# Attention's group ends spread over three steps, output products between its last transposes, and a reordered start of the gate products

## The chip, the cores and the metric

The kernel runs on one core of a Trainium2 chip. A core has five engines with an instruction queue each: TensorE (matrix products and transposes; the profile calls it PE, and its weight loads PEld), VectorE (DVE), ScalarE (ACT), GpSimd (POOL) and SyncE (SP, which here issues DMAs). Each engine works through its queue in order, and waits where an operand or a buffer is not ready. The metric is the device time of one execution in microseconds (us); the median of several runs is compared.

## The reference

The program computes one layer of a hybrid encoder block in float32, on 1024 tokens of width 1024:

```python
h = rms_norm(x, norm1_g)
a, gate, q, k, v = split(h @ w_in)                  # 512 columns each
conv_out = silu(layer_norm(depthwise_conv31(a * sigmoid(gate)) + dw_bias))
q, k = rms_norm per head (8 heads of 64) of q, k
attn_out = neighbourhood_attention(q, k, v, rpb)    # 16 x 64 token grid, window 8 rows x 16 columns
x = x + concat([conv_out, attn_out]) @ w_out
h = rms_norm(x, norm2_g)
out = x + (silu(h @ w_gate) * (h @ w_up)) @ w_down  # hidden width 2816
```

## The kernel before

Every large product is made from two rounded parts of each operand. `split(hi, lo, src, sub)` lets ScalarE write the rounded copy `hi`, and then the engines in `sub` write the remainder `lo = src - hi`, each an equal share of the columns; GpSimd is the default. `mac` (lines 110 to 114) then runs three matrix products on TensorE: hi with hi, hi with lo, lo with hi. The order of the work is written out by hand: each function issues instructions, and each engine takes its own in that order. A list `woven` holds functions that are called one by one between the products of a running accumulation (`weave`).

**Attention** works in 32 steps, one pair of heads of one query block each; four steps make a group (`order`), a group has one half of the rows (`rh`) and one block of 16 columns (`cb`). The loop (from line 775) is a software pipeline. Step i makes the scores of pair i (`score_mm`, TensorE; `score_exp`, VectorE and ScalarE), scales the exponentials of pair i - 1 (`score_norm`: reciprocal on VectorE, scaling on GpSimd), transposes those of pair i - 2 (`flip`, into the one buffer `cv` of PSUM, emptied by `flip_out`: one half by ScalarE, then the other by VectorE), and multiplies the transposed ones of pair i - 3 with the values (`weigh`, into `os_`, one bank for a group, two such banks). When the fourth pair of a group has been weighed (step 6, 10, 14, ...), `evac` splits the group's output into `at`, ScalarE first and then VectorE. Columns of the groups are 24 wide at first (288 scores a row) and 32 wide from step 16 (384 scores).

Beside this, `take_parts` cuts the split of a piece of output weights `wo` into four quarters, `jobs`, one called at the end of every second step: ScalarE's rounded copy and GpSimd's remainder. `take` does a whole piece at once. After the fourth quarter the next piece is loaded (SyncE's queue).

At step 32, `attn_half(0)` runs the four attention blocks (k = 4 to 7) of the output product of token block 0, 12 matrix products in a row, ahead of the last two transposes. After the loop follow the convolution's transposes `conv_T` (the first into `cv`), the rest of the output products, and `conv_stats`, which takes means and variances on VectorE, in part with operations on 128x1 numbers (lines 739 and 747).

**From the output product to the gate.** The second half of the output product runs over eight token blocks t (from line 984): products, `resid(t, 1)` (VectorE adds the residual), `norm2(t)` (a DMA of the sum, ScalarE's square and root). Woven into the next block's products are `norm2_out(t - 1)` (VectorE scales to `xn`), the transposes `t2_one` with their splits into `h2`, and `s_sum`.

The gate and up products are made by a Strassen scheme: seven products m1 to m7 of half-sized blocks for each of 22 blocks i (`FB`), instead of eight. `s_sum(t, ns, eng)` makes the sums S1, S2 (`sn`) and, in place, S3 and S4 (in `xn`) of the tokens; `t_sums` those of the weights on VectorE; `s_T` transposes and splits a sum of the tokens into four blocks. `prep` takes the next (i, p) of `tasks`, makes the weight's sum where needed, splits it (remainder on GpSimd) and issues loads of later weights. `product(i, p)` runs 12 matrix products; `evac(i, p, acc)` empties or combines the result. Three products share bank A or B or D: m2 of a block goes into the bank that its m1 used, so it waits for the copy of m1 into `g` (line 1020, ScalarE). The first two blocks are interleaved: m1 of block 0, m1 of block 1, m2 of block 0, m2 of block 1, then m6, m5, m7, m4, m3 in the same way. After the eighth token block and ahead of the first product stand `norm2_out(7)`, an activation that makes ScalarE load the table for Silu (line 995), `s_sum(3, (1, 2), dve)` and one `prep`.

Of the kernel before, what the change touches and what calls it, by code (L numbers as in the profile page):

```python
# [6 lines left out]
F32 = mybir.dt.float32  # L7
# [60 lines left out]
def build(ctx, tc, a):  # L68
# [25 lines left out]
    def mm(name):  # L94
        return ps.tile([P, 512], F32, tag="mm", bufs=4, name=name)
# [7 lines left out]
    def split(hi, lo, src, sub=(pool,)):  # L103
        act.copy(hi, src)  # L104
        n = src.shape[-1] // len(sub)
        for i, eng in enumerate(sub):
            sl = slice(i * n, (i + 1) * n)
            eng.tensor_tensor(*[w[..., sl] for w in (lo, src, hi.bitcast(F32))], OP.subtract)  # L108
# [8 lines left out]
    woven = []  # L117
# [71 lines left out]
    def wo_dst(d, k0):  # L189
        def dst():  # L190
            if (d, k0 // 4) not in woq:
                woq[d, k0 // 4] = H(f"wo{d}{k0}", F32R)
            q = woq[d, k0 // 4]
            o = k0 % 4 * 1024
            hl = (q[:, o:o + 1024], q[:, o + 1024:o + 2048])
            for j in range(2):
                wo[d, k0 + j] = [w[:, j * 512:(j + 1) * 512] for w in hl]
            return hl
        return dst

    for d in range(2):
        for k0 in (4, 6, 0, 2):
            want(a["wo"][k0 * P:(k0 + 2) * P, d * 512:(d + 1) * 512].rearrange("(k p) m -> p k m", p=P),
                 f"wo{d}{k0}", wo_dst(d, k0))


    hT = [[H(f"hT{h}{w}", F32R).rearrange("p (k s) -> p k s", s=512) for w in range(2)] for h in range(2)]
# [442 lines left out]
    def weigh(i):  # L650
        s_, hp = divmod(i, 4)
        rh, cb = order[s_]
        if hp == 0:
            os_[s_] = tp(f"o{s_}").rearrange("p (c q) -> p c q", c=4)
        for g in range(3):
            for hh in range(2):
                c = (2 * hp + hh) * HD
                pe.matmul(os_[s_][hh * HD:(hh + 1) * HD, hp], vw[cb, rh + g][:, c:c + HD], pTs[i][:, g, hh],  # L658
                          start=g == 0, stop=g == 2)

    def evac(s_):
        rh, cb = order[s_]
        o = os_.pop(s_)
        if rh == 0:
            at[cb] = [G(f"at{cb}{w}", F32R).rearrange("p (c t q) -> p c t q", c=4, t=2) for w in range(2)]
        split(*[w[:, :, rh] for w in at[cb]], o, (dve,))

    def value(t):
        z = nat(2, t)
# [42 lines left out]
    def proj(t, d, acc, ks):  # L712
        for k in ks:
            mac(acc, lhs(k, t), wo[d, k], k == 4, k == 3)
            weave()

    def conv_T(t):
        y = cv(f"y{t}")[:, :512] if t in (0, 3) else tp(f"y{t}")
        for c in range(4):
            pe.transpose(y[:, c * P:(c + 1) * P], u[c][0][:, t * P:(t + 1) * P], ident)  # L720
        return y
# [3 lines left out]
    def conv_stats(t, y):  # L725
        st6, mv, sd = SM(f"bs{t}", 6), SM(f"bm{t}", 2), SM(f"bd{t}", 1)
        dve.bn_stats(st6, y)
        dve.bn_aggr(mv, st6)
        act.activation(sd, mv[:, 1:2], AF.Sqrt, bias=eps)
        cs[t] = y, mv, sd  # L730
        if 1 <= t <= 4:
            conv_scale(t - 1)
        if t >= 4:
            conv_scale(t)
# [36 lines left out]
    def attn_half(t):  # L771
        acc0.append(mm(f"pj{t}"))
        proj(t, 0, acc0[t], range(4, 8))

    for i in range(2, 32 + 2):
        if i == 5:
            tab[0, 1] = tab[0, 2] = table(0, 1)
        if i == 9:
            tab[1, 1] = tab[1, 2] = table(1, 1)
        if i in (6, 12):  # L780
            load_window(i // 6)
        if i in (14, 22):
            take_parts(jobs)
        if i < 32:
            ss = score_mm(i)
        if i == 32:
            act.activation(warm, eps, AF.Sqrt)
            attn_half(0)
        if i < 33:
            score_norm(i - 1)  # L790
        flip(i - 2)
        flip_out(i - 2, 1)
        if i < 32:
            score_exp(i, ss)
        flip_out(i - 2, 0)
        if i > 2:
            weigh(i - 3)
            if i % 4 == 2:
                evac(i // 4 - 1)
        if jobs and i % 2 == 0:  # L800
            jobs.pop(0)()

    cm += [H(f"cm{w}", F32R).rearrange("p (k s) -> p k s", s=S) for w in range(2)]
    conv_stats(0, conv_T(0))
    woven.extend([lambda: (weigh(31), evac(7)), lambda: conv_stats(1, conv_T(1)), lambda: None])
    for t in range(2, 8):
        woven.extend([lambda t=t: conv_stats(t, conv_T(t)), lambda: None])
    take()
# [38 lines left out]
    def norm2_out(t):  # L847
        r = SM(f"r2{t}r", 1)
        dve.reciprocal(r, sd2[t])
        xn[t] = G(f"xn{t}")  # L850
        dve.scalar_tensor_tensor(xn[t], x2[t], r, g2b, OP.mult, OP.mult)
# [34 lines left out]
    def prep(n=1):  # L886
        for _ in range(n):
            if not tasks:
                return
            i, p = tasks.pop(0)  # L890
            if i < 2:
                if i == 1 and p in ("m6", "m5"):
                    t_sums(i, (1, 2) if p == "m6" else (3, 4))
            elif p == "m1":
                t_sums(i, (1, 2))
            elif p == "m6":
                t_sums(i, (3, 4))
            b = {"m1": (0, 0), "m2": (0, 1), "m3": (1, 1)}.get(p)
            n = {"m5": 0, "m6": 1, "m7": 2, "m4": 3}.get(p)
            src = lr(raw_gu[i, b[0]])[b[1]] if b else lr(tsum[i, n // 2])[n % 2]  # L900
            top[i, p] = lr(G(f"t{i}{p}", F32R))
            split(*top[i, p], src)
            if (i, p) == (0, "m2"):
                load_gu(1, 1)
            if (i, p) == (1, "m5"):
                load_gu(2, 0)
            if (i, p) == (0, "m3"):
                load_gu(2, 1)
            if (i, p) == (1, "m3"):
                load_gu(3, 0)  # L910
            if i > 1 and p == "m2":
                load_gu(i + 1, 1)
            if i > 1 and p == "m3":
                load_gu(i + 2, 0)
# [40 lines left out]
    def s_weave(n):  # L955
        skip = lambda: None
        parts = [lambda kb=kb: s_T(n, kb) for kb in range(3)]
        woven.extend([skip, skip, parts[0], skip, parts[1], parts[2]] if n == "S2" else
                     [parts[0], skip, parts[1], skip, parts[2]])

    g2b = G("g2b")
# [22 lines left out]
    for t in range(8):  # L984
        for n in range(KB):
            woven.append(lambda fs=beside.get(t, {}).get(n, ()): [f() for f in fs])
        acc = mm(f"pk{t}")
        proj(t, 1, acc, (4, 5, 6, 7, 0, 1, 2, 3))
        unravel()
        resid(t, 1, acc)  # L990
        norm2(t)
        if t in (3, 4, 5):
            prep()
    norm2_out(7)
    act.activation(warm, eps, AF.Silu)
    s_sum(3, (1, 2), dve)
    prep()
    sop["A11"], sop["A12"] = ([[w[:, o + k] for k in range(HK)] for w in h2] for o in (0, HK))

    sd = dr.tile([QF, P, 7 * 512], F32, name="sd")  # L1000
# [14 lines left out]
    def evac(i, p, acc):  # L1015
        if p == "m1":
            gt[i] = G(f"g{i}")
        l, r = lr(gt[i])
        if p == "m1":
            act.copy(l, acc)  # L1020
        elif p == "m6":
            u2[i] = ST(f"u2{i}")
            dve.tensor_tensor(u2[i], acc, l, OP.add)  # L1023
        elif p == "m2":
            sl[i] = ST(f"sl{i}") if i < 2 else acc
            act.activation(sl[i], acc, AF.Silu)  # L1026
        elif p == "m5":
            dve.tensor_tensor(r, acc, l, OP.add)  # L1028
        elif p == "m7":
            dve.tensor_tensor(r, acc, r, OP.add)  # L1030
        elif p == "m3":
            dve.tensor_tensor(l, acc, l, OP.add)
            dve.tensor_tensor(l, sl[i], l, OP.mult)
            keep(i, 0, l)
        else:
            dve.tensor_tensor(acc, acc, u2[i], OP.add)  # L1036
            act.activation(acc, acc, AF.Silu)  # L1037

            def f():
                dve.tensor_tensor(r, acc, r, OP.mult)  # L1040
                keep(i, 1, r)
            late.append(f)
# [91 lines left out]
    for n, (i, p) in enumerate(products):  # L1134
        if i == 0 and p in NEXT:
            s_weave(NEXT[p])
        acc = product(i, p)
        if 1 <= n < 9:
            s_sum((n - 1) % 4, (3 + (n > 4),), pool)
        evac(i, p, acc)  # L1140
        if late and p != "m4":
            late.pop(0)()
        if extra and p in ("m2", "m5", "m7", "m6"):
            extra.pop(0)()
        prep()
        if i == FB - 1 and p in ("m2",):
            for q in range(4):
                load_item(q)
        if i == FB - 1 and p in ("m5", "m7", "m3", "m4"):
            prep_items(1)  # L1150
# [90 lines left out]
```

## Time and profile before

| | us |
|---|---|
| median of 3 runs (1074.04 to 1075.7) | 1075.66 |
| profiled execution | 1074.17 |
| its span, first to last instruction | 1072.4 |
| TensorE busy | 1048.1 (98%) |
| VectorE busy | 698.4 (65%) |
| ScalarE busy | 452.3 (42%) |
| GpSimd busy | 390.2 (36%) |

The granted TensorE clock was 0.995 over the span. In a time line, a row has the start in us from the span's start, the length, the engine, the line of the kernel, the operation, what it writes and reads with shapes, the count of merged instructions, and in brackets the idle time of the engine just before and what ended it. In a list of waits, a row says who waited for whom, then the total in us, the number of times and the longest. TensorE's records overlap, since its matrix products are pipelined: the distance from start to start is what one costs.

### The profile page before, as it was taken

How to read it: one execution, taken by the hardware profiler on the slowest of the kernel's cores; microseconds unless marked ns; L12 is line 12 of the kernel's file. 1: busy time of each engine (PE TensorE's matmuls, PEld its weight loads, DVE VectorE, ACT ScalarE, POOL GpSimd, SP SyncE). 2: the span in 40 equal slices, each digit the busy share in tenths (PEclk: the TensorE clock that was granted, in tenths of full speed). 3: DMA queues.
4: the chain of work that ended last, by engine and by line, in shares of the span. 5: the costliest groups of instructions: out<-in, count | busy, mean ns of one | idle time of the engine just before them, and what ended most of it. 6: DMA issues, size and time to landing. Idle time of an engine off the chain costs nothing.

```text
span 1072.4 us, 14055 instructions
## 1 busy us (share of the span) xinstructions
PE 1048.1 (98%) x5068; PEld 849.9 (79%) x5068; DVE 698.4 (65%) x1055; ACT 452.3 (42%) x988; POOL 390.2 (36%) x303
## 2 busy tenths in 40 slices
PE   7999999989999999999999999999999999999997
PEld 6888888866667888788888888888888888888886
DVE  6778997885765336765646555564555567858873
ACT  6455358725775423533222333223232344433441
POOL 0136665513552301844454544544544300002310
PEclk9999999999999999999999999999999999999999
DMA  9426781244413422123332323323232497634641
GB/s 339 155 55 215 229 245 40 74 150 140 152 57 105 156 103 90 40 89 108 120 107 69 130 96 108 108 98 99 98 128 79 169 339 277 206 95 127 205 129 43
DMA packets 68245, 144.06 MB, mean 134 GB/s; under 512 B 12496, under 2 KB 21200, under 8 KB 67536
## 3 DMA queue, kind: packets, MB, share of 16 engines
q1 hardware_dynamic: 66336, 139.95, 38.8%
q10 hardware_dynamic: 1840, 3.22, 0.9%
q8 instruction: 40, 0.66, 0.3%
q14 instruction: 29, 0.24, 0.1%
HBM read 103.99 MB, written 44.76 MB: 139 GB/s over the span
## 4 chain that ended last, share of the span: by engine, by line
PE 88%; DVE 5%; ACT 3%; issue 2%; DMA 1%; POOL 1%; SPq 0%; ACTq 0%; DVEq 0%; POOLq 0%
PE B L113 6%; PE B L114 6%; PE B L112 6%; PE D L114 4%; PE D L112 4%; PE D L113 4%; PE A L112 4%; PE A L114 4%; PE A L113 4%; DVE cv L319 3%; PE gl L114 3%; PE gl L113 3%; PE gl L112 3%; PE z L112 2%; PE z L114 2%; PE z L113 2%
## 5 line engine op out<-in xcount | busy, mean ns | idle before, releaser
L319 DVE SCALAR_TENSOR_TENSOR cv<-u,par,cv 128x1009 f32<-128x1009 f32 (+14 forms) x92 | 117.5, 1277 | 2.5
L345 POOL TENSOR_TENSOR pa<-pa,pr 128x1022 f32<-128x1022 f32 (+5 forms) x24 | 57.5, 2398 | 51.3 <-ACT pr L344 47.4
L104 ACT CAST op<-sr 128x512 fp32r<-128x512 f32 x77 | 47.6, 619 | 52.4 <-PE B2d L114 26.6
L1028 DVE TENSOR_TENSOR g<-B,g 128x512 f32<-128x512 f32 x22 | 15.2, 691 | 79.1 <-PE B L114 79.1
L108 DVE TENSOR_TENSOR op<-sr,op 128x512 fp32r<-128x512 f32 x77 | 55.6, 722 | 17.1 <-ACT op L104 17.1
L1196 POOL TENSOR_TENSOR ou<-ou,resm 128x512 f32<-128x512 f32 x8 | 11.5, 1446 | 145.2 <-DMA resm<-xd 145.2
L1037 ACT ACTIVATE D<-D 128x512 f32<-128x512 f32 x22 | 12.8, 582 | 113.1 <-DVE D L1036 113.1
L1023 DVE TENSOR_TENSOR u<-B,g 128x512 f32<-128x512 f32 x22 | 15.2, 690 | 62.1 <-PE B L114 62.1
L104 ACT CAST op<-wd 128x512 fp32r<-128x512 f32 x66 | 40.9, 619 | 30.5 <-DVE wd L1115 18.2
L877 DVE TENSOR_TENSOR ts<-gu,ts 128x512 f32<-128x512 f32 x44 | 53.1, 1206 | 0.8
L633 POOL TENSOR_SCALAR e<-e,rs 128x288 f32<-128x288 f32 (+1 forms) x64 | 34.2, 547 | 52.2 <-DVE rs L631 38.0
L108 DVE TENSOR_TENSOR op<-wd,op 128x512 fp32r<-128x512 f32 x66 | 50.3, 762 | 1.6
L1026 ACT ACTIVATE A<-A 128x512 f32<-128x512 f32 x20 | 11.6, 582 | 76.3 <-PE A L114 76.3
L626 ACT ACTIVATE e<-e,mx 128x288 f32<-128x288 f32 (+1 forms) x64 | 36.2, 568 | 14.8 <-DVE mx L624 14.8
L642 PEld LDWEIGHTS p<-ident,e 128*96 128x96 f32 (+1 forms) x192 | 20.0, 133 | 18.6 <-issue 10.3
L877 DVE TENSOR_TENSOR ts<-gu 128x512 f32<-128x512 f32 x22 | 34.4, 1566 | 0.0
L624 DVE CUSTOM_DVE_ANT_0 e<-s,tab 128x288 f32<-128x288 f32 (+1 forms) x64 | 29.8, 502 | 7.1 <-PE s L611 6.7
L611 PE MATMUL s<-kT,qT 64*128 64x288 f32 (+1 forms) x128 | 28.1, 500 | 4.6 <-DVE mx L624 4.6
L642 PE MATMUL p<-ident,e 128*96 128x128 f32 (+1 forms) x192 | 27.5, 279 | 3.8 <-DVE pT L647 2.5
L372 ACT ACTIVATE sq<-z,r 128x64 f32<-128x64 f32 x96 | 28.6, 334 | 2.2 <-PE z L114 2.2
L658 PE MATMUL o<-pT,vw 96*64 96x128 f32 (+1 forms) x384 | 28.0, 281 | 0.0
L344 ACT ACTIVATE pr<-u,par 128x1022 f32<-128x1022 f32 (+5 forms) x24 | 27.0, 1138 | 1.6 <-ACT vs L403 1.6
(1034 smaller groups left out, 3459.2 us busy)
## 6 DMA issues: line engine op xcount, KB each, us to landing
gu<-in_gu SPq DMA_DIRECT2D x44, 512.0 KB
sr<-sd SPq DMA_DIRECT2D x77, 256.0 KB
sd<-sd SPq DMA_DIRECT2D x22, 512.0 KB
wd<-in_wd SPq DMA_DIRECT2D x44, 256.0 KB
sd<-g SPq DMA_DIRECT2D x33, 256.0 KB
x<-in_x SPq DMA_DIRECT2D x16, 512.0 KB
xd<-x SPq DMA_DIRECT2D x8, 512.0 KB
resm<-xd SPq DMA_DIRECT2D x16, 256.0 KB
```

Source lines behind the costliest of these rows:

```text
L104: act.copy(hi, src)
L108: eng.tensor_tensor(*[w[..., sl] for w in (lo, src, hi.bitcast(F32))], OP.subtract)
L112: pe.matmul(acc, lh, rh, start=start, stop=False, skip_group_check=True)
L113: pe.matmul(acc, lh, rl, start=False, stop=False, skip_group_check=True)
L114: pe.matmul(acc, ll, rh, start=False, stop=stop, skip_group_check=True)
L319: dve.scalar_tensor_tensor(acc[:, o], uc[:, i], dwk[:, c, t:t + 1], acc[:, o], OP.mult, OP.add)
L345: pool.tensor_tensor(pa[:, o], pa[:, o], pr[:, o], OP.add)
L624: dve.tensor_tensor_reduce(out=e[:, hh], in0=ss[hh], in1=tab[rh, cb][2 * hp + hh], scale=-1.0, scalar=3.0e38, op0=OP.add, op1=OP.min, accu ...
L626: act.activation(e[:, hh], e[:, hh], AF.Exp, bias=mx, scale=-1.0, accum_out=rs[:, hh:hh + 1])
L633: pool.tensor_scalar(es[i][:, hh], es[i][:, hh], rs[:, hh:hh + 1], 1.0, op0=OP.mult, op1=OP.mult)
L642: pe.transpose(pt[:m, g * P:(g + 1) * P], es[i][:, hh, g * m:(g + 1) * m], ident)
L877: dve.tensor_tensor(o, l, r, OP.subtract)
```

## The change

In attention, `evac` becomes two functions: `evac_hi`, ScalarE's copy of the whole group, in the place of `evac`; and `evac_lo`, VectorE's remainder, called for one half of the group's columns at the end of each of the next two steps. The quarters of output weights are called at steps 0 and 1 of every four in place of every second step. The 12 products of `attn_half(0)` become `fill`: six in their old place, three before the last transposes and three after the loop. Two pieces of `wo` get their remainder in four parts on GpSimd. After attention, one more `prep` goes in front of the eighth token block's products; the remainders of the first two blocks' m1, m2, m6 and m5 go to VectorE; `norm2_out(7)`, the Silu activation and `s_sum(3, ...)` come after the first product; block 0's copy of m1 goes to VectorE; the transposes of S2 all come into the product m2 of block 1; GpSimd's `s_sum` come later in the program, and so do two of the `prep`.

```diff
-                 f"wo{d}{k0}", wo_dst(d, k0))
+                 f"wo{d}{k0}", wo_dst(d, k0), (pool,) * 4 if d == 0 and k0 < 4 else (pool,))
...
-    def evac(s_):
+    def evac_hi(s_):
         rh, cb = order[s_]
-        o = os_.pop(s_)
         if rh == 0:
             at[cb] = [G(f"at{cb}{w}", F32R).rearrange("p (c t q) -> p c t q", c=4, t=2) for w in range(2)]
-        split(*[w[:, :, rh] for w in at[cb]], o, (dve,))
+        act.copy(at[cb][0][:, :, rh], os_[s_])
+
+    def evac_lo(s_, cs=slice(0, 4)):
+        rh, cb = order[s_]
+        hi, lo = [w[:, cs, rh] for w in at[cb]]
+        dve.tensor_tensor(lo, os_[s_][:, cs], hi.bitcast(F32), OP.subtract)
...
+    def fill(*ks):
+        if not acc0:
+            act.activation(warm, eps, AF.Sqrt)
+            acc0.append(mm("pj0"))
+        proj(0, 0, acc0[0], ks)
...
-        if i == 32:
-            act.activation(warm, eps, AF.Sqrt)
-            attn_half(0)
+        if i >= 32:
+            fill(*((4, 5) if i == 32 else (6,)))
...
             if i % 4 == 2:
-                evac(i // 4 - 1)
-        if jobs and i % 2 == 0:
+                evac_hi(i // 4 - 1)
+            elif i > 6 and i % 4 in (0, 3):
+                evac_lo((i + 1) // 4 - 2, slice(0, 2) if i % 4 == 3 else slice(2, 4))
+        if jobs and i % 4 < 2:
             jobs.pop(0)()
+    fill(7)
...
-    woven.extend([lambda: (weigh(31), evac(7)), lambda: conv_stats(1, conv_T(1)), lambda: None])
+    woven.extend([lambda: (weigh(31), evac_hi(7), evac_lo(7)), lambda: conv_stats(1, conv_T(1)), lambda: None])
...
-            split(*top[i, p], src)
+            split(*top[i, p], src, (dve,) if i < 2 and p in ("m1", "m2", "m6", "m5") else (pool,))
...
-        woven.extend([skip, skip, parts[0], skip, parts[1], parts[2]] if n == "S2" else
+        woven.extend([skip, skip, skip, skip, parts[0], parts[1], parts[2]] if n == "S2" else
...
-        if t in (3, 4, 5):
+        if t in (3, 4, 5, 6):
             prep()
-    norm2_out(7)
-    act.activation(warm, eps, AF.Silu)
-    s_sum(3, (1, 2), dve)
-    prep()
...
-            act.copy(l, acc)
+            (act.copy if i else dve.tensor_copy)(l, acc)
...
         acc = product(i, p)
-        if 1 <= n < 9:
-            s_sum((n - 1) % 4, (3 + (n > 4),), pool)
+        for t in {3: (0, 1), 4: (2, 3), 5: (4,), 6: (5,), 7: (6,), 8: (7,)}.get(n, ()):
+            s_sum(t % 4, (3 + t // 4,), pool)
         evac(i, p, acc)
+        if n == 0:
+            norm2_out(7)
+            act.activation(warm, eps, AF.Silu)
+            s_sum(3, (1, 2), dve)
...
-        prep()
+        prep({1: 0, 2: 0, 3: 2, 5: 2}.get(n, 1))
```

## The prediction

> **What bounds the kernel now.** I read the first part of the page, then TensorE's waits, then the time lines of the stretches that hold those waits: attention's loop (235 to 331 us of the span) and the first gate products (425 to 450 us). The first fence is the page's busy line and, from the list of waits (total us, times, longest), TensorE's.
>
> ```profile
> PE 1048.1 (98%) x5068; PEld 849.9 (79%) x5068; DVE 698.4 (65%) x1055; ACT 452.3 (42%) x988; POOL 390.2 (36%) x303
> PE p L642 <- DVE pT L647: 2.5, 5, 0.6
> PE A L112 <- ACT g L1020: 2.1, 1, 2.1
> PE p L642 <- POOL e L633: 1.3, 3, 0.5
> ```
>
> TensorE is busy 98% of a span of 1072.4 us. It computes the same products after the change, so the change can win only waits of TensorE, and loses only where it makes new ones. The three waits above are 5.9 us; the change works on all three.
>
> The next fence is one of attention's waits: first VectorE's time line, then TensorE's (start, length, what, and in brackets the idle time before it with its releaser).
>
> ```profile
> 295.73 0.17 DVE L631 RECIPROCAL rs<-rs 128x2 f32<-128x2 f32 x1 [0.65 <-ACT e L626]
> ...
> 296.98 0.56 DVE L647 COPY pT<-p 128x384 f32<-128x384 f32 x1
> 298.73 0.69 DVE L108 TENSOR_TENSOR at<-o,at 128x512 fp32r<-128x512 f32 x1 [1.19 <-ACT at L104]
> 299.33 0.15 DVE L631 RECIPROCAL rs<-rs 128x2 f32<-128x2 f32 x1
> ```
>
> ```profile
> 299.63 0.92 PE L611 MATMUL s<-kT,qT 64*128 64x384 f32 x4
> 301.05 0.85 PE L642 MATMUL p<-ident,e 128*128 128x128 f32 x6 [0.50 <-DVE pT L647]
> ...
> 305.09 0.92 PE L611 MATMUL s<-kT,qT 64*128 64x384 f32 x4
> 305.93 0.33 PE L642 MATMUL p<-ident,e 128*128 128x128 f32 x1
> ```
>
> In the step after a group's fourth head pair VectorE stands 1.19 us waiting for ScalarE's rounded copy of the group's output, because the remainder (`at`, L108) is next in its queue. The reciprocal, the two score additions and the copy of the transposes stand behind it, and TensorE's next transposes wait for that copy: they start 1.42 us after the scores (299.63 to 301.05), where an undisturbed step has 0.84 (305.09 to 305.93). So one group end costs 0.58 by the starts, 0.50 by the label.
>
> **The change, part by part.**
>
> *Group ends in attention.* The evac becomes ScalarE's copy in its old place, and two half remainders on VectorE, at the ends of the next two steps. Seven group ends lie in the loop. The last (step 30) is followed by output products that hide it, so six pay. The two rows of waits for `p` have 2.5 + 1.3 = 3.8 us in eight waits; one is the loop's first (0.6, the longest of the row), one is the tail's (0.50, below); six remain with 2.7 us. With the 0.08 by which the start-to-start count exceeds the label, they are 2.7 + 6 x 0.08 = 3.2. What takes their place: ScalarE's copy remains, but nothing of VectorE waits for it in its step. A half remainder costs between half of the 0.69 row (0.35) and all of it; I take 0.4, near the half, since it reads half as much. Its cover is VectorE's idle time ahead of the reciprocal, 0.65 in the row quoted, when the copy of the transposes is already done. If that cover were gone, 14 halves x 0.4 = 5.6 us would land on TensorE. The quarters of output weights move from even steps to steps 0 and 1 of each four; what they queue past is GpSimd's normalisation:
>
> ```profile
> 304.04 0.73 POOL L108 TENSOR_TENSOR wo<-wo06r,wo 128x256 fp32r<-128x256 f32 x1 [1.24 <-ACT wo L104]
> 304.75 1.14 POOL L633 TENSOR_SCALAR e<-e,rs 128x384 f32<-128x384 f32 x2
> ```
>
> It ends at 304.75 + 1.14 = 305.89 and the transposes start at 305.93: on time with nothing to spare, in a step with such a quarter and without a group end. Eight quarters instead of four in undisturbed steps risk hundredths each. I take 3.1 for this part, bounds 1.5 (below, a rival) and 3.5. The DMA that the fourth quarter issues goes out one step later and is for weights of the projection's second half, with the whole first half between: nothing.
>
> *Products between the last transposes.* TensorE's rows at the loop's end:
>
> ```profile
> 323.22 0.81 PE L642 MATMUL p<-ident,e 128*128 128x128 f32 x6
> 323.96 0.88 PE L658 MATMUL o<-pT,vw 128*64 128x128 f32 x12
> 325.34 0.84 PE L642 MATMUL p<-ident,e 128*128 128x128 f32 x6 [0.50 <-DVE pT L647]
> 326.12 0.88 PE L658 MATMUL o<-pT,vw 128*64 128x128 f32 x12
> 327.40 0.66 PE L720 MATMUL y<-ident,u 128*128 128x128 f32 x4 [0.41 <-DVE pT L647]
> ```
>
> Twelve output products stand ahead of 323.22; the change leaves six there and puts three into each of the two gaps. A product takes 0.23 (two starts in the PE rows further down, 430.31 and 430.53), three take 0.68. Transposes to transposes is now 325.34 - 323.22 = 2.12; without the gap 0.74 + 0.81, with three products 2.23, more than the wait needed. Transposes to `y` is 2.06; with them 0.78 + 0.81 + 0.68 = 2.27. So six fewer ahead (-1.37) and 0.11 + 0.21 in place of the gaps: 1.05 saved; I take 0.9, since ScalarE's table load for the root, ahead of the copies, now has only six products beside it. Bounds 0.4 and 1.05.
>
> *GpSimd's two remainders of output weights in quarters.* GpSimd, VectorE and TensorE where the second runs:
>
> ```profile
> 335.88 2.38 POOL L108 TENSOR_TENSOR wo<-wo02r,wo 128x1024 fp32r<-128x1024 f32 x1 [3.13 <-ACT wo L104]
> ...
> 337.40 0.88 DVE L747 SCALAR_TENSOR_TENSOR bb<-bm,br 128x1 f32<-128x1 f32 x1
> ...
> 339.88 0.66 PE L720 MATMUL y<-ident,u 128*128 128x128 f32 x4 [0.29 <-ACT xh L748]
> ```
>
> The 128x1 operation lasts 0.88, to 338.28, when GpSimd's 2.38 end (338.26); ScalarE's `xh` and TensorE's 0.29 follow from it. Against quarters (0.73 in the row above) it would wait at most 0.73, on average half of that. Four quarters take 4 x 0.73 = 2.92 in place of 2.38, on an engine that nothing waits for here. I take 0.2 gained, bounds 0 and 0.29.
>
> *The first gate products.* ScalarE's, VectorE's, TensorE's and GpSimd's rows:
>
> ```profile
> 430.44 1.28 ACT L995 ACT_TABLE_LOAD   x1
> 431.73 0.20 ACT L995 ACTIVATE warm<-eps 128x1 f32<-128x1 f32 x1
> 431.84 0.60 ACT L104 CAST t1m<-gu 128x512 fp32r<-128x512 f32 x1
> 432.35 0.58 ACT L1020 COPY g<-A 128x512 f32<-128x512 f32 x1
> ```
>
> ```profile
> 422.85 1.29 DVE L108 TENSOR_TENSOR h<-t,h 128x512 fp32r<-128x512 f32 x2 [2.02 <-ACT h L104]
> 424.06 0.68 DVE L928 TENSOR_TENSOR sn<-xn 128x512 f32<-128x512 f32 x1
> ...
> 428.23 0.68 DVE L767 TENSOR_TENSOR x<-pk,x 128x512 f32<-128x512 f32 x1
> ```
>
> ```profile
> 430.31 0.39 PE L113 MATMUL A<-h,t1m 128*128 128x512 f32 x1
> 430.53 0.39 PE L114 MATMUL A<-h,t1m 128*128 128x512 f32 x1
> 432.98 0.50 PE L112 MATMUL A<-h,t0m 128*128 128x512 f32 x1 [2.06 <-ACT g L1020]
> ...
> 440.39 0.39 PE L112 MATMUL B<-S,t0m 128*128 128x512 f32 x1
> ```
>
> ```profile
> 432.52 1.28 POOL L108 TENSOR_TENSOR t1m<-gu,t1m 128x512 fp32r<-128x512 f32 x1 [16.15 <-ACT t1m L104]
> ```
>
> Call E the end of VectorE's last residual sum, here 428.23 + 0.68 = 428.91. m2 of block 0 goes into the bank that m1 of block 0 leaves, and that copy stands on ScalarE behind the square, the root, the table load, `warm` and a rounded copy: m2 starts at E + 4.07 (432.98). The change gives this copy to VectorE: m2 could start about 0.7 (a 512-column VectorE operation, 0.68 in the residual's row) after E. But the copy for block 1 stays on ScalarE, behind the same chain with one rounded copy in it, so block 1's m2 cannot start before E' + 4.1, where E' is E in the new kernel. Block 0's m2 takes 12 x 0.23 = 2.74 and would be through at E' + 3.4: a new wait of 0.7. All 16 transposes of S2 now stand in block 1's m2. From 432.98 to the first `B` product are 7.41 us here; without block 0's 2.74 they are 4.67. So this product starts at E' + 8.77, where it started at E + 11.48: the gain is 2.71 less the delay of E.
>
> What delays E: two of the first three remainders fall into idle time of VectorE, together about 0.3. The fourth (m2, block 1) is new there and goes in front of the two `h` remainders, for which VectorE waited 2.02: it waits as long, for its own rounded copy, and then adds its 0.7. Last, GpSimd. It stood idle for 16.15 us up to 432.52, and its next instruction was held by a rounded copy. With these remainders on VectorE there is nothing ahead of the sums in its queue: they come later in the program, and earlier in time, each as soon as VectorE has made the S2 sum that it follows. Block 0's will run one residual step earlier and block 1's behind VectorE's `sn` (424.06 here, some 1.5 later in the new kernel), 1.28 each by the last row, at the moment when VectorE wants to scale `xn` from two SBUF operands. By the rows at 335.88 and 337.40 such an operation stands until GpSimd's ends. I take 0.5 for the first (VectorE first has an operation from PSUM to do) and 1.2 for the second. Delay of E: 0.3 + 0.7 + 0.5 + 1.2 = 2.7, gain 0.0. Behind it two preparations come two products later than now, so that VectorE's differences for block 1 stand just ahead of the products that need them: 0.2 lost. This part: 0.2 slower, bounds 2.06 gained (the whole wait) and 1.5 lost (the second collision, and half of that again).
>
> The table load has a rule against this change. The Trainium skill, "ScalarE: Activation LUTs", section "What ACT_TABLE_LOAD costs", gives 1283 ns for the load and about 1380 ns for a drain, 2.66 us for each switch. By the page the chain to block 1's copy would be 1.38 us longer and this part 1.6 lost instead of 0.2. The trace shows 1.28 and the next operation 0.01 later (430.44 + 1.28 = 431.72, then 431.73): the load agrees, the drain is not there, and the measured row is used.
>
> *Elsewhere* the same weights are loaded, summed and multiplied; from the third block on nothing is changed.
>
> **The sum.** 3.1 + 0.9 + 0.2 - 0.2 = 4.0 us. The profiled execution took 1074.17 (its span and 1.77 around it): 1070.2. The runs shown have two levels, this one and 1.49 above it, where the median of 1075.66 stands; I put the prediction half way up, at 1070.9.
>
> **Rivals.**
>
> *The collision does not come*, because GpSimd's sums fall beside operations from PSUM. Then E is delayed by 1.0 and the gate part gains 2.71 - 1.0 - 0.2 = 1.5. The total is 5.7: 1069.2. For it: only two operations collide. Against: both sums become ready just as VectorE turns to those operations.
>
> *Attention's waits change hands.* GpSimd's normalisation ends the wait three times of the eight (the 1.3), and the quarter ahead of it has no slack. If eight steps with a quarter lose 0.2 each, that part gains 1.5 and the total is 2.4: 1072.5. For it: 305.89 against 305.93. Against: the quoted step is such a step and lost nothing.
>
> *Slower: the halves are not covered.* If a half costs the whole 0.69 (a price by instruction, not by column) and VectorE's chain, reciprocal to copy, has no room, 14 x 0.69 = 9.7 come back in attention: 1080.6. It cancels the 4.0 from 0.29 uncovered in each half, and makes the kernel slower by 0.2% from 0.44. For it: the reciprocal stands at the head of that chain. Against: the 0.65 idle ahead of it.
>
> *The change of the table load's page*: 1.4 more, 1072.3; the row at 431.73 leaves it no chance of its own.
>
> **How the numbers follow.** My forecast 0.50, no collision 0.22, waits that change hands 0.14, halves not covered 0.06, anything that I do not see 0.08. About 0.2% (2.1 us) is what a measurement of this kernel can tell from no change. The first two are faster, the third lies about at this border, the others are the same or slower: faster 0.74, same 0.14, slower 0.12. Range: below, no collision with the whole 2.06 and the bounds of attention (3.5 + 1.05 + 0.29 + 2.06 = 6.9 off the profiled 1074.17) is 1067.3; above, waits that change hands with the gate's 1.5 lost, from the upper level of the runs, is 1074.6. I give 1067.5 to 1074.2.
>
> **What would show it.** Right: in attention no remainder of `at` in front of a reciprocal, transposes 0.84 after the scores in every step, the two rows of `p` down to about 0.6 in sum; no wait of `y` for the copies; the 128x1 operation under 0.9. At the gate: the wait for `g` moved from block 0's m2 to block 1's, some 0.7 us; the first of GpSimd's sums before the first gate product, with the `xn` operation beside it well above its length of today. Wrong: a longer row of `p` waits on GpSimd or VectorE, or sums on GpSimd that begin only after the first products.

## The result, and the profile after

The changed kernel takes 1070.09 us as a median (1069.13 to 1071.14), the kernel before 1075.68 beside it; the ratio is 0.9952, with a 95% interval of 0.9942 to 0.9961. It is 0.5% faster. The prediction said 1070.9 in a range of 1067.5 to 1074.2. Two single executions in the experiments took 2709.62 and 2960.06 us, a slow state, and are left out of every median and ratio.

TensorE's waits in the changed kernel (total us, times, longest):

```profile
PE z L112 <- ACT wk0h L104: 6.5, 1, 6.5
PE s L611 <- DVE mx L624: 4.6, 1, 4.6
PE B L113 <- DVE S L108: 0.9, 1, 0.9
PE gl L114 <- POOL ag10l L108: 0.6, 1, 0.6
PE p L642 <- DVE pT L647: 0.6, 1, 0.6
PE A L112 <- DVE g L1028: 0.5, 1, 0.5
PE A L112 <- ACT g L1028: 0.3, 1, 0.3
```

Of the rows shown before, `p` waits once for VectorE (the loop's first step, as before) and never for GpSimd; the 2.1 of `A` has become 0.5 and 0.3; and `B` has a new 0.9. The rows of `z` and `s` belong to the program's start and to the loop's first steps.

To see where the time went, I read from each trace the starts of the same few operations of TensorE and took the distances between them (us). The loop runs from the start of the third pair's scores (246.28 in the kernel before) to that of the last (317.90); the tail to the first transposes of the convolution (327.40); the projection to the first gate product (425.32); B is the first product of bank B (440.39), D the first of bank D (455.25), both counted from the first gate product.

| kernel | loop | tail | projection | to B | to D | D to the end |
|---|---|---|---|---|---|---|
| before | 71.62 | 9.50 | 97.92 | 15.07 | 29.93 | 617.15 |
| changed | 68.65 | 8.67 | 97.60 | 14.02 | 30.31 | 617.20 |
| difference | -2.97 | -0.83 | -0.32 | -1.05 | +0.38 | +0.05 |

The sum without the column of B, which D contains, is -3.69; with the loop's start, 0.11 earlier, it is the -3.8 between the spans (1072.4 and 1068.6). The medians of the runs differ by 5.6, which is 1.8 more than the traces account for. The two kernels' runs scatter by 2 us each, the start of the loop alone lies between 244.8 and 246.7 in the traces of this study, and in three later series the kernel before had medians of 1075.01, 1074.46 and 1075.19, so 1075.68 is on the high side. The distances are the sharper measure, and the small terms below are read from them. Each kernel has one trace: a term of a few tenths counts where several kernels with the same code there agree.

*The group ends.* VectorE, then TensorE, in a step after a group's fourth pair:

```profile
297.48 0.56 DVE L647 COPY pT<-p 128x384 f32<-128x384 f32 x1 [0.15 <-ACT pT L647]
297.96 0.41 DVE L670 TENSOR_TENSOR at<-o,at 128x256 fp32r<-128x256 f32 x1
298.68 0.17 DVE L631 RECIPROCAL rs<-rs 128x2 f32<-128x2 f32 x1 [0.31 <-ACT e L626]
```

```profile
297.61 0.92 PE L611 MATMUL s<-kT,qT 64*128 64x384 f32 x4
298.46 0.88 PE L642 MATMUL p<-ident,e 128*128 128x128 f32 x6
```

A half remainder takes 0.41, behind the copy, and VectorE still stands idle 0.31 before the reciprocal. The transposes follow the scores after 0.85.

*The tail.* The last two groups of transposes and the first of the convolution, with products between them that are left out here:

```profile
318.77 0.82 PE L642 MATMUL p<-ident,e 128*128 128x128 f32 x6
...
321.12 0.82 PE L642 MATMUL p<-ident,e 128*128 128x128 f32 x6
...
323.49 0.60 PE L724 MATMUL y<-ident,u 128*128 128x128 f32 x4
```

The distances are 2.35 and 2.37, without a wait; they were 2.12 and 2.06 with six products more ahead of them.

*The quarters of the remainders.* GpSimd's four quarters and the 128x1 operation that meets the first of them:

```profile
331.92 2.82 POOL L108 TENSOR_TENSOR wo<-wo02r,wo 128x256 fp32r<-128x256 f32 x4 [2.71 <-ACT wo L104]
```

```profile
332.01 0.66 DVE L751 SCALAR_TENSOR_TENSOR bb<-bm,br 128x1 f32<-128x1 f32 x1
```

No transpose of the convolution waits in the list above.

*The gate.* VectorE's operation that makes `xn` in the kernel before; the two of the changed kernel that are longer, and GpSimd's sum beside the second; then the starts of m2 of the two blocks:

```profile
425.57 1.29 DVE L851 SCALAR_TENSOR_TENSOR xn<-x,r26r,g2b 128x1024 f32<-128x1024 f32 x1
```

```profile
414.13 1.53 DVE L863 SCALAR_TENSOR_TENSOR xn<-x,r25r,g2b 128x1024 f32<-128x1024 f32 x1
...
422.24 2.12 DVE L863 SCALAR_TENSOR_TENSOR xn<-x,r26r,g2b 128x1024 f32<-128x1024 f32 x1
```

```profile
421.54 1.73 POOL L940 TENSOR_TENSOR xn<-xn,xn 128x512 f32<-128x512 f32 x1 [6.97 <-DVE sn L940]
```

```profile
427.15 0.47 PE L112 MATMUL A<-h,t0m 128*128 128x512 f32 x1 [0.45 <-DVE g L1028]
...
430.48 0.50 PE L112 MATMUL A<-h,t1m 128*128 128x512 f32 x1 [0.34 <-ACT g L1028]
```

GpSimd's sums, later in the program, run earlier than before (its first sum of the tokens stood behind a remainder that began at 432.52), and the two operations that they meet grow from 1.28 to 1.53 and 2.12. The wait of m2 is shared between the blocks.

### The profile page after: what moved, and what is told of

Its sections match the earlier page's. It is cut to its first block, busy times and chain, and to the rows that moved or that the text cites. A ratio compares the mean times of both kernels' runs of the same rounds, so it can differ in the third digit from the quotient of the medians.

```text
span 1068.6 us, 14069 instructions
## 1 busy us (share of the span) xinstructions
PE 1048.0 (98%) x5068; PEld 849.4 (79%) x5068; DVE 704.9 (66%) x1071; ACT 451.3 (42%) x987; POOL 383.2 (36%) x301
## 4 chain that ended last, share of the span: by engine, by line
PE 89%; DVE 6%; issue 1%; ACT 1%; DMA 1%; POOL 0%; SPq 0%; DVEq 0%; POOLq 0%; ACTq 0%
PE B L113 5%; PE B L114 5%; PE B L112 5%; PE D L114 4%; PE D L112 4%; PE D L113 4%; PE A L112 3%; PE A L114 3%; PE A L113 3%; DVE cv L319 3%; PE gl L114 3%; PE gl L112 3%; PE gl L113 3%; PE z L112 2%; PE z L113 2%; PE z L114 2%
```

## The experiments

All are compared by the distances of the table. The halves made twice, the old quarters, the whole remainders, the later table load and the earlier differences were executed once each; their times are not compared, only their distances. The theory was that of the prediction: attention's waits go, and the gate part moves its waits rather than removing them. The rivals: the waits of attention change hands, or the gate part pays.

**The group ends alone** (with the quarters' new steps), on the kernel before:

```diff
-                evac(i // 4 - 1)
-        if jobs and i % 2 == 0:
+                evac_hi(i // 4 - 1)
+            elif i > 6 and i % 4 in (0, 3):
+                evac_lo((i + 1) // 4 - 2, slice(0, 2) if i % 4 == 3 else slice(2, 4))
+        if jobs and i % 4 < 2:
```

> The kernel before with one part of the change: the group ends in three steps and the quarters of output weights in steps 0 and 1 of four. My theory: the six group ends stop delaying TensorE's transposes; scores to transposes is 0.84 us in all the wide steps, the last scores start 3.0 us earlier than before (the changed kernel has 3.0 there), the two waits at the loop's end (0.50 and 0.41) stay, and the program ends 2.8 to 3.1 earlier. Rival (the waits change hands): new waits of p on GpSimd of 0.1 to 0.3 a step, 1.5 gained. Rival (given back later): 3.0 at the last scores and less than 2 at the end.

The ratio was 0.9971 (0.9959 to 0.9982). The loop took 68.65, exactly what it takes in the changed kernel, and no wait of `p` but the loop's first and the tail's was left. But the projection took 99.07 where the kernel before has 97.92: 1.15 were given back, which no theory had expected at that place. By the distances it is the second rival that came: 3.0 at the last scores, 1.8 at the first gate product. The medians, 1071.77 against 1075.01, differ by 3.2, with an interval of the ratio that allows 1.9 to 4.4; they cannot decide it. TensorE's wait, then GpSimd and VectorE there:

```profile
PE y L724 <- ACT xh L752: 1.5, 1, 1.5
```

```profile
332.18 2.38 POOL L108 TENSOR_TENSOR wo<-wo02r,wo 128x1024 fp32r<-128x1024 f32 x1 [3.11 <-ACT wo L104]
```

```profile
332.26 2.31 DVE L751 SCALAR_TENSOR_TENSOR bb<-bm,br 128x1 f32<-128x1 f32 x1
```

An operation on 128x1 numbers, 0.16 when it is free, lasts 2.31 us: GpSimd began 0.08 before it, and it ends with GpSimd. In the kernel before, the operation of the same token block came 0.24 ahead of GpSimd's (335.88) and was free:

```profile
335.64 0.16 DVE L747 SCALAR_TENSOR_TENSOR bb<-bm,br 128x1 f32<-128x1 f32 x1
```

There it was the next block's (337.40, in the prediction) that met GpSimd, 1.5 us into its operation, and the loss was 0.29. So a shift of 0.32 us decides which operation is caught, and the group ends had made it; how they did, the traces do not settle.

**Attention's three parts without the gate's**: the changed kernel up to the gate, the kernel before from there.

> The changed kernel with everything from the gate on as before: group ends, products between the last transposes, quartered remainders. My theory: attention's three parts give 3.0 + 0.9 + 0.3 = 4.2 us ahead of the first gate product, and all of it lasts to the end, so this is 0.3 to 0.5 faster than the changed kernel, whose own gate part loses 0.4 between the first gate product and the first product of bank D. Rival (the gate part pays): this kernel ends later than the changed one by 1 us or more.

The distances are 68.65, 8.67, 97.64, then 15.07 and 29.95: each part has what it has in the changed kernel or in the one before. Up to D the 4.1 last; from D to the end it takes 617.42, which is 0.27 more than in the kernel before and at the upper end of what that stretch takes in the traces (617.14 to 617.42). The ratio of 0.9961 (0.9946 to 0.9976) cannot be told from the changed kernel's 0.9952; by the distances this kernel is 0.36 ahead of it at D and 0.1 at the end. The rival, 1 us later or more, falls.

**The gate part alone**: the kernel before up to the gate, the changed kernel from there.

> The kernel before with the gate part alone. My theory: m2 of block 0 starts 1.6 earlier, the first product of B 1.0 earlier, and the first product of bank D 0.4 later than before, since the waits come back at m2 of block 1 (0.5) and at m5 of block 0 (about 1); the time is the same within what can be told, 0.0 to 0.6 longer. Rival (the gate part pays): the wait of 2.06 goes and nothing comes for it, 1.5 to 2 faster.

Ratio 0.9992 (0.9982 to 1.0002): the same. B comes 13.99 after the first gate product and D 30.31, as in the changed kernel. The first gate products gain 1.05 to 1.08, and 1.43 to 1.46 are lost between B and D. The gate part does not pay.

**GpSimd's sums held back**, on the changed kernel:

```diff
-            split(*top[i, p], src, (dve,) if i < 2 and p in ("m1", "m2", "m6", "m5") else (pool,))
+            split(*top[i, p], src, (dve,) if i < 2 and p in ("m1", "m2", "m6", "m5") and (i, p) != (0, "m6") else (pool,))
```

> The changed kernel with one remainder, block 0's m6, back on GpSimd: it waits there for its rounded copy, made after the table load, so GpSimd's sums of the tokens, which stand behind it, cannot start before the gate. My theory (collision): the two operations that make xn, 1.53 and 2.12 us in the changed kernel, are 1.28 again; VectorE's last residual sum ends 1.0 to 1.1 earlier, m2 of block 0 waits for nothing, m2 of block 1 starts 0.9 to 1.1 earlier. What lasts of it depends on the sums, which now run beside VectorE's work for block 1: 0.3 to 1.0 at the first product of bank D. Rival (the chain of ScalarE alone sets the start): m2 of block 1 starts within 0.2 of where it did.

The collision was real: the two operations that make `xn` take 1.28 and 1.29 again, m2 of block 0 starts 5.44 after the first gate product (6.06 in the changed kernel), without a wait, and m2 of block 1 8.31 after it (9.39), 1.08 earlier. But nothing of it lasts: D comes at 30.33. I had expected 0.3 to 1.0. VectorE and GpSimd, where it is lost:

```profile
435.97 1.38 DVE L889 TENSOR_TENSOR ts<-gu,gu 128x512 f32<-128x512 f32 x1
```

```profile
430.08 5.47 POOL L940 TENSOR_TENSOR xn<-xn,xn 128x512 f32<-128x512 f32 x4
435.51 1.29 POOL L940 TENSOR_TENSOR xn<-xn,sn 128x512 f32<-128x512 f32 x1
```

The sums now run into block 1's weight differences: the first of these lasts 1.38 instead of 0.68. The second difference ends 17.10 after the first gate product (17.12 in the changed kernel), and what is behind it on VectorE is as late as before.

**Halves made twice**, on the changed kernel: how much room is left behind the copies.

```diff
-        dve.tensor_tensor(lo, os_[s_][:, cs], hi.bitcast(F32), OP.subtract)
+        for _ in range(2):
+            dve.tensor_tensor(lo, os_[s_][:, cs], hi.bitcast(F32), OP.subtract)
```

> The changed kernel with each half remainder of attention made twice (the same values written again). My theory: a half is covered by VectorE's idle time before the next reciprocal, so the second half, some 0.34 from start to start, uses what is left of it: 0 to 1.5 us in all over 14 halves, between the loop's first and last scores. Rival (the halves are not covered, the chain from reciprocal to copy has no room): all of the 14 x 0.34 = 4.8 us shows there.

The loop took 68.66 and the tail 8.65: a second half costs nothing there. The rival by which the halves would make the kernel slower falls. (The projection grew by 0.38; the last group's remainder, whole and made twice too, stands there ahead of the convolution's statistics.)

**The quarters at every second step again**, on the changed kernel:

```diff
-        if jobs and i % 4 < 2:
+        if jobs and i % 2 == 0:
```

> The changed kernel with the quarters of output weights at every second step again, so that four of them fall in the steps of the group ends. My theory: there ScalarE has its copy of the group and the quarter's rounded copy (0.57 + 0.41) ahead of its copy of the transposes, so those steps take 0.0 to 0.2 longer each, 0 to 0.8 us in the loop; the halves on VectorE are what removed the waits. Rival (the quarters' new steps are what removed them): waits of p of 1.3 or more in the loop.

The loop took 69.12, 0.47 more, in the steps after a group end with a quarter. So of the 2.97 some 2.5 come from the remainders and 0.5 from the quarters' places; the waits did not change hands.

**The two remainders of output weights whole again**, on the changed kernel:

```diff
-                 f"wo{d}{k0}", wo_dst(d, k0), (pool,) * 4 if d == 0 and k0 < 4 else (pool,))
+                 f"wo{d}{k0}", wo_dst(d, k0))
```

> The changed kernel with the two remainders of output weights whole again on GpSimd. My theory: which of the two engines is first at the shared port is decided by some hundredths of a us; with the group ends spread, GpSimd's 2.4 us operation starts first, a 128x1 operation of VectorE lasts 2 us or more, and a transpose of the convolution waits 1.0 to 1.6 us more, as in the kernel with the group ends alone. Rival (the quarters bring only what they brought before, 0.3): the wait is 0.3 or less.

The projection took 99.02, 1.42 more, and the transposes waited 1.46:

```profile
333.97 0.66 PE L724 MATMUL y<-ident,u 128*128 128x128 f32 x4 [1.46 <-ACT xh L752]
```

So the quarters, 0.32 better than the kernel before, are worth 1.4 once the group ends are spread.

**The table load behind block 1's copy**, on the changed kernel:

```diff
             norm2_out(7)
-            act.activation(warm, eps, AF.Silu)
...
+        if n == 1:
+            act.activation(warm, eps, AF.Silu)
```

> The changed kernel with the activation that makes ScalarE load the Silu table behind block 1's copy of m1, instead of ahead of it. My theory: that copy waits only for ScalarE's chain, so without 1.28 + 0.2 in it m2 of block 1 waits for nothing (it waited 0.3, 0.5 by the starts), and the first product of B comes 0.2 to 0.5 earlier; nothing of it is left at the first product of bank D, because the later wait for VectorE's remainders of S1 takes it. If a load cost 2.66 as the page of the tables has it, m2 of block 1 would not have waited so little in the changed kernel. Rival (S2's sums set m2 of block 1): no difference at B.

m2 of block 1 starts 8.87 after the first gate product (9.39), B 13.42 (14.02), and D 29.73 (30.31). The 0.60 at B is a little above the 0.2 to 0.5 expected; that 0.58 of it would last was not expected at all. The transposes of S2 move with m2, and with them VectorE's work on S2: its last remainder of S2 starts 13.97 after the first gate product (14.57), at the head of the chain that D waits for.

**Block 1's weight differences earlier**, on the changed kernel:

```diff
-                if i == 1 and p in ("m6", "m5"):
-                    t_sums(i, (1, 2) if p == "m6" else (3, 4))
+                if (i, p) == (1, "m5"):
+                    t_sums(1, (3, 4))
...
-        woven.extend([skip, skip, skip, skip, parts[0], parts[1], parts[2]] if n == "S2" else
+        woven.extend([skip, skip, skip, skip, parts[0], lambda: (parts[1](), t_sums(1, (1, 2))), parts[2]] if n == "S2" else
```

> The changed kernel with block 1's first two weight differences moved to between the transposes of S2, where VectorE stood idle for 1.30, instead of behind them. My theory: these two (0.68 each) and the rounded copy that waits for them head the chain on VectorE that ends with the remainder of S1's last two blocks, for which m5 of block 0 waits 0.9; so the waits at m6 of block 1 and m5 of block 0 (together 1.4 from the first product of B to that of D) go down by 1.0 to 1.4, and the program ends that much earlier. Rival (the wait comes from GpSimd, which holds the port ahead of the remainder of m5, 1.77 long): that operation stays at 1.7 and the gain is under 0.4.

B is at 14.05, as it was; D at 28.66: 1.65 earlier than in the changed kernel and 1.27 earlier than in the one before. The wait of `B` for VectorE is gone from the list. More than the expected 1.0 to 1.4 came; the remainder of m5 no longer meets GpSimd, which no run separates from the rest. First the changed kernel, then this one, each with the remainder of S1's last two blocks behind it:

```profile
443.11 1.77 DVE L108 TENSOR_TENSOR t1m<-ts,t1m 128x512 fp32r<-128x512 f32 x1
444.80 1.21 DVE L108 TENSOR_TENSOR S<-sp,S 128x1024 fp32r<-128x1024 f32 x1
```

```profile
440.04 0.69 DVE L108 TENSOR_TENSOR t1m<-ts,t1m 128x512 fp32r<-128x512 f32 x1
440.65 1.22 DVE L108 TENSOR_TENSOR S<-sp,S 128x1024 fp32r<-128x1024 f32 x1
```

Counted from the first gate product, the last remainder of S1 ends at 24.92 in the changed kernel and at 22.06 here. So the theory (the differences head the chain) holds, and the port of its rival had a part: the operation did not stay at 1.7, because it came 1.79 earlier and GpSimd's remainder (442.66, here 440.95) only 0.43.

**Both edits together**, the best version:

> The changed kernel with both edits: the table load behind block 1's copy of m1, and block 1's first two weight differences between the transposes of S2. My theory: the first came to 0.58 and the second to 1.65 at the first product of bank D, by two different waits, so together 2.0 to 2.3 earlier than the changed kernel from the first gate product on; about 1067.5 to 1068.5 as a median, 0.6 to 0.7% under the kernel before. Rival (both shorten the same chain): no more than the 1.65 of the second.

> The same kernel as in the run named best, for its trace: by my theory m2 of block 1 starts 8.8 to 8.9 after the first gate product, the first product of B 13.4 after it, and the first of bank D 28.0 to 28.7 after it (30.3 in the changed kernel, 29.9 in the one before). By the rival (one chain) the last is 28.6 or 28.7.

Two series of runs gave medians of 1067.67 and 1067.78 us, with ratios of 0.9935 (0.9921 to 0.9948) and 0.9937 (0.9921 to 0.9954) against the kernel before. In its trace B is at 13.41 and D at 28.03, 2.28 earlier than in the changed kernel: the two gains add up (0.58 + 1.65). TensorE's waits there:

```profile
PE z L112 <- ACT wk0h L104: 6.5, 1, 6.5
PE s L611 <- DVE mx L624: 4.6, 1, 4.6
PE p L642 <- DVE pT L647: 0.6, 1, 0.6
PE A L112 <- DVE g L1028: 0.5, 1, 0.5
```

Besides the program's start and the loop's first steps, only the wait for block 0's copy is left, with the collision at `xn` ahead of it.

**The sums held back in the best version** (the edit of the experiment above on it):

> The one before this with block 0's m6 remainder on GpSimd, so that the sums are held until the gate. My theory: m2 of block 0 waits for nothing (0.6 earlier, as when the sums were held in the changed kernel), but the sums then run beside the weight differences, which each stand for up to 1.3: between 0.6 gained and 1.0 lost at the first product of bank D. Rival (the hold pays in full here): 0.6 or more gained there.

1070.3 us, 0.9956 (0.9940 to 0.9971): worse than without. m2 of block 0 waits for nothing (5.44), but D is at 30.34, 2.3 later. The sums stand beside four of VectorE's operations:

```profile
428.37 1.66 DVE L940 TENSOR_TENSOR sn<-xn 128x512 f32<-128x512 f32 x1
430.07 1.63 DVE L940 TENSOR_TENSOR sn<-sn,xn 128x512 f32<-128x512 f32 x1
...
434.48 1.41 DVE L889 TENSOR_TENSOR ts<-gu,gu 128x512 f32<-128x512 f32 x1
435.92 1.67 DVE L889 TENSOR_TENSOR ts<-gu,ts 128x512 f32<-128x512 f32 x1
```

This was below the range I had given (0.6 gained to 1.0 lost): the two sums that make S2 were not in my count.

## Why the prediction was right, and where its terms were off

*Group ends:* 3.1 expected, 2.97 measured, in the loop with the whole change and with this part alone. The price of a half (0.4, measured 0.41) and its cover held; there was even room for a second half. One term was at nothing: the new places of the quarters counted only as a risk, and they bring 0.5 of the 2.97.

*Tail:* 0.9 expected, 0.83 measured.

*Quarters of the remainders:* 0.2 expected, 0.32 measured between the two kernels. The step was too small in another way, and that it came out near was luck: I took the loss in the kernel before as its price, though that loss depends on where the two engines meet. With the group ends spread and the remainders whole it is 1.4.

*Gate:* 0.2 slower expected, 0.38 slower measured, but by two errors that nearly cancel; that number was luck. The step "delay of E: 2.7" was too large. VectorE's last residual sum ends at 426.41 (425.73 and 0.68), the first gate product starts 4.23 earlier than before, so E is delayed by 426.41 + 4.23 - 428.91 = 1.73. The collisions cost 0.25 and 0.84 (1.53 and 2.12 against 1.28), where I had put 0.5 and 1.2, and the remainders on VectorE cost the other 0.64, where I had put 1.0. The rest of the step held: m2 of block 1 starts 4.07 after E' (4.1 expected), B 8.70 after it (8.77 expected). So B gains 1.05 and not 0.0. And the step "0.2 lost" behind it was too small: B to D takes 16.29 in place of 14.86, 1.43 lost. I had seen that the differences stand just ahead of their products, but priced the wait and not the chain behind it. In the kernel before the first of them starts 8.95 after the first gate product (434.27), in the changed one 15.71 (436.80), although GpSimd stretches four of these differences before (1.60 to 1.78 for 0.68) and none after. Moving the first two alone gives back 1.65.

*The rivals.* Waits that change hands and halves that are not covered are excluded by the loop's 68.65 and 68.66. That the collision does not come is excluded by the two rows of `xn` and by the sums held back, which moves m2 of block 1 by 1.08. What its absence would bring is shown only in part: with the sums held back B comes 1.77 earlier than in the kernel before (13.30 against 15.07), as that rival has it (2.71 - 1.0), but nothing of it is left at D. There the held sums stretch another operation of VectorE, and a kernel without either collision was not run.

*The table load.* In the changed kernel ScalarE's root ends at 427.91, the load runs from 427.94 to 429.22, and the next operation starts at 429.23. The trace has no room on either side for the drain of about 1380 ns that the Trainium skill, "ScalarE: Activation LUTs", section "What ACT_TABLE_LOAD costs", adds to a load.

*The time itself.* The sum of 4.0 stands against 3.8 between the spans. The forecast of 1070.9 is 0.8 above the measured median; where between the two levels of the runs it should stand was a choice, and no run explains the levels.

## What to carry to other kernels

A wait that is taken from the engine that bounds the kernel is worth its length only up to the next thing that is late, so count the chain behind a moved preparation to its end, through every queue, and not only the wait at its head. Moving an instruction later in the program does not make it run later: an engine whose queue is empty ahead of it starts it as soon as its operands are there, and a neighbour on a shared port pays. Where a short operation on the critical chain can meet a long one of another engine, cut the long one: it is a price against chance, and it grows when anything else shifts.

## What was not expected of the hardware

An operation of VectorE on 128x1 numbers with two operands in SBUF lasted 0.16, 0.88, 2.31 or 0.66 us in the traces: alone, behind the rest of a GpSimd operation of 2.38, behind nearly all of it, and behind a quarter of it. Between the kernel before and the one with the group ends alone VectorE shifted against GpSimd by 0.32 us: from 0.24 ahead of GpSimd, with 0.16 for that operation, to 0.08 behind it, with 2.31. The Trainium skill, "SBUF — State Buffer", section "SBUF: two separate sides", says that of a GpSimd operation and a VectorE operation with two inputs in SBUF the one that starts first gets the shared pair of ports for the whole instruction and the other fully blocks. The rows agree with it: the 0.88 ends at 338.28 and GpSimd's operation at 338.26, the 2.31 at 334.57 and GpSimd's at 334.56.
